# Feed-forward gate by seven block products instead of eight, in a two-layer decoder block

## The chip, the core and the metric

The kernel runs on one core of one Trainium2 chip. The metric is the device time of one execution in microseconds (us). Of three runs of the kernel before, the median is 2764.52 us (2763.65 to 2766.2). The engines are TensorE (PE in the profile; its weight loads PEld), VectorE (DVE), ScalarE (ACT), GpSimd (POOL) and SyncE (SP), which issues every load and store of this kernel on one queue (SPq).

## The reference, cut to what matters

Two decoder layers over 256 tokens with 2048 channels: a token mixer (retention in layer 0, a convolution module in layer 1), a feed-forward part, and a gated per-layer embedding. The change concerns the feed-forward part, which both layers have:

```python
def swiglu(hn, w_gate, w_up, w_down):
    return (jax.nn.silu(hn @ w_gate) * (hn @ w_up)) @ w_down

# in each layer i, h is (256, 2048), FFN_HIDDEN = 5632:
f = swiglu(rms_norm(h, g_ffn_pre[i]), ffn_w_gate[i], ffn_w_up[i], ffn_w_down[i])
h = h + rms_norm(f, g_ffn_post[i])
```

## The kernel before, in words

Everything is float32 at the boundary. Each operand of a matrix product is split into a high part, rounded to the reduced type fp32r, and a low part (the value minus the high part, again fp32r), and a product is three matmuls (`mm3`, L119 to L122): high by high, high by low, low by high. The weights come from memory as tiles of 256 rows by 512 columns (512 KB, `st`, four buffers). `wload` (L75 to L85) issues the load on SP, copies it to the high part `wh` on ACT (L79) and subtracts to the low part `wl` on DVE (L84); `wh` and `wl` have eight buffers each. The activations lie transposed in SBUF as stationary operands: quarters of 4 x 128 channels, high and low, for both token tiles (TT = 2 tiles of 128 tokens), which class `Act` hands out.

`gemm` (L131 to L176) makes 512 output columns for both token tiles: eight weight tiles of two K tiles each, for each K tile both token tiles, three matmuls for each, so 16 x 2 x 3 = 96 matmuls of 128x128 by 128x512. With `outer=True` it goes through all K for token tile 0 first and then for token tile 1 with the weights kept, so that the second tile's activations may come later. Hooks put other work behind a given weight tile.

`ffn` (L588 to L628) walks the 5632 hidden columns in eleven blocks of 512, in groups of 3, 4 and 4 blocks. For each block it makes the gate product, evicts it with a Silu on ACT (L603), makes the up product, multiplies on DVE (L607), transposes the result on TensorE and splits it (`split_to`, L105) into the hidden activations. After each group the down product goes over the group's hidden columns for each of four blocks of 512 outputs: the first group is copied to `y` on ACT (L498), the second added on DVE (L624), the last one added, squared and summed, and scaled (`make_final`, L525). The residual stream `ht` (eight tiles of 128x512) stays in SBUF in a pool `hp` from the end of the retention mixer to the end of the kernel.

Accumulators in PSUM: four tiles `acc`, two for transposes `tp`, two `sm` for the small products. The order of the instructions on each engine is not that of the text: the framework schedules them at compile time, by program order as the priority and by when it reckons that an operand or a buffer is there. Each engine, and the SP queue, then runs its own list strictly in order and waits on semaphores.

Of the kernel before, what the change touches and what calls it, by code (L numbers as in the profile page):

```python
# [10 lines left out]
F32 = mybir.dt.float32  # L11
# [6 lines left out]
P = 128  # L18
# [23 lines left out]
def block_kernel(ctx: ExitStack, tc: tile.TileContext, x, p, positions, w_in, w_out, w_pw1, b_pw1,  # L42
# [76 lines left out]
    def mm3(ps, xh, xl, wh, wl, first, last):  # L119
        nc.tensor.matmul(ps, lhsT=xh, rhs=wh, start=first, stop=False)  # L120
        nc.tensor.matmul(ps, lhsT=xh, rhs=wl, start=False, stop=False)  # L121
        nc.tensor.matmul(ps, lhsT=xl, rhs=wh, start=False, stop=last)  # L122
# [8 lines left out]
    def gemm(act, w, k0, c0, nkt, name, outer=False, hooks=None, on_done=None, hooks1=None, pair=None):  # L131
# [44 lines left out]
        return acc  # L176

# [396 lines left out]

    ssqs = post_setup()
    for c in range(NC):
        if c == 1:
            ret.close()
            hp = ctx.enter_context(tc.tile_pool(name="hp", bufs=1))
            for tt in range(TT):  # L580
                for cc in range(NC):
                    t = ht[tt, cc] = hp.tile([P, CW], F32, tag=f"h{tt}{cc}", name=f"h{tt}{cc}")
                    nc.sync.dma_start(t, x[0, tt * P:(tt + 1) * P, cc * CW:(cc + 1) * CW])
        gemm(yT[1], wo, D, c * CW, NKT, "wo", outer=(c == NC - 1), hooks=hk if c == 0 else None,
             on_done=make_final(c, ssqs, g_mix_post[0], ret_after))


    def ffn(layer, s_hid, after):  # L588
        wg, wu, wd = w_gate[layer], w_up[layer], w_down[layer]
        es = ExitStack()  # L590
        fp = es.enter_context(tc.tile_pool(name=f"ffn{layer}", bufs=1))
        f0 = 0
        groups = (3, 4, 4)
        ssqs = post_setup()
        for gi, n in enumerate(groups):
            hid = Act(s_hid, f"hid{layer}{gi}")
            for j in range(n):
                c0 = (f0 + j) * CW
                sgs, hids = {}, {}

                def gate_done(tt, ps):
                    sgs[tt] = fp.tile([P, CW], F32, tag=f"sg{tt}", name="fsg")
                    nc.scalar.activation(sgs[tt], ps, AF.Silu, scale=rf[layer, tt])  # L603

                def up_done(tt, ps):
                    hids[tt] = fp.tile([P, CW], F32, tag=f"hid{tt}", name="fhid")
                    nc.vector.scalar_tensor_tensor(hids[tt], ps, rf[layer, tt], sgs[tt], op0=ALU.mult, op1=ALU.mult)  # L607

                gemm(fa[layer], wg, 0, c0, NKT, "fg", outer=(gi == 0 and j == 0), on_done=gate_done,
                     hooks={0: pend} if j > 0 else None)  # L610
                gemm(fa[layer], wu, 0, c0, NKT, "fu", on_done=up_done)

                def pend(j=j, hids=hids, hid=hid):
                    for tt in range(TT):
                        split_to(hid, j, tt, transpose4(hids[tt]))
            for c in range(NC):
                last = gi == len(groups) - 1
                if last:
                    done = make_final(c, ssqs, g_ffn_post[layer], after)
                elif gi == 0:  # L620
                    done = first_group_done(c)
                else:
                    def done(tt, ps, c=c):
                        nc.vector.tensor_tensor(y[tt, c], ps, y[tt, c], op=ALU.add)  # L624
                gemm(hid, wd, f0 * CW, c * CW, 4 * n, "fd", outer=(last and c == NC - 1),
                     on_done=done, hooks={1: pend} if c == 0 else None)
            f0 += n
        es.close()  # L628
# [277 lines left out]
    ple(1, final_out)  # L906

# [74 lines left out]
```

## Time and profile before

| | |
|---|---|
| median of three runs | 2764.52 us |
| the profiled execution's own time | 2762.31 us |
| its span, first to last instruction | 2760.5 us |
| PE busy | 2726.0 us (99%), 12288 matmuls |
| DVE busy | 1548.9 us (56%) |
| ACT busy | 1248.4 us (45%) |
| DMA | 521.76 MB, mean 189 GB/s |
| granted TensorE clock | 0.997 of full speed |

A row of a group of instructions reads: line, engine, operation, output and inputs by the program's names, shapes, count; then busy time in us and mean duration of one in ns; then the idle time of that engine just before them and what ended it. Matmuls are pipelined: one shows as 0.39 us and the next begins before it ends, so that the distance from start to start is what one costs. A row of a table of stretches has the stretch and its length, then for each engine busy time and count, then the granted clock, the DMA engines' mean busy share and the rate in GB/s.

### The profile page before, as it was taken

What the parts mean: (1) busy time and instruction counts of PE and PEld (TensorE: products, weight loads), DVE (VectorE), ACT (ScalarE), POOL (GpSimd) and SP (SyncE); (2) the same over time, 40 slices, a digit from 0 to 9 for tenths busy, and PEclk for the clock granted to TensorE, in tenths of its full rate; (3) what the DMA queues carried; (4) which work ended last, traced back from release to release, by engine and by line L of the source; (5) the groups of instructions that cost most, each with busy time, mean ns of one, the idle gap of its engine ahead of it and who ended that gap; (6) DMA issues with size and microseconds to landing.
All of it is one profiled execution on the core that took longest, in us unless ns stands there. A gap on an engine that the chain in (4) does not pass through costs nothing. (4 is left out here: it accounts for less than half of the span.)

```text
span 2760.5 us, 32081 instructions
## 1 busy us (share of the span) xinstructions
PE 2726.0 (99%) x12288; PEld 2249.9 (82%) x12288; DVE 1548.9 (56%) x1701; ACT 1248.4 (45%) x1498; POOL 36.7 (1%) x45
## 2 busy tenths in 40 slices
PE   9999999999999999999999999989999999999998
PEld 7888888888888888888888877878888888888877
DVE  7655545555565445454456577766554445454564
ACT  5444444444454444434444554465444443444453
POOL 0000000000000000000000000000000000000000
PEclk9999999999999999999999999999999999999999
DMA  8666566666576666566655665545756665666653
GB/s 265 195 179 181 183 194 183 181 180 202 168 221 192 190 191 187 192 194 190 189 199 168 206 205 167 163 152 183 226 190 191 191 189 192 192 190 191 202 183 122
DMA packets 293082, 521.76 MB, mean 189 GB/s; under 512 B 18156, under 2 KB 61004, under 8 KB 292928
## 3 DMA queue, kind: packets, MB, share of 16 engines
q1 hardware_dynamic: 292928, 519.72, 60.5%
q8 instruction: 96, 1.57, 0.2%
q14 instruction: 58, 0.48, 0.1%
HBM read 517.55 MB, written 2.10 MB: 188 GB/s over the span
## 5 line engine op out<-in xcount | busy, mean ns | idle before, releaser
L84 DVE TENSOR_TENSOR wl<-st,wh 128x1024 fp32r<-128x1024 f32 x944 | 1154.2, 1224 | 1076.3 <-ACT wh L79 1071.8
L79 ACT CAST wh<-st 128x1024 fp32r<-128x1024 f32 x944 | 993.4, 1053 | 1286.1 <-PE fu L122 268.6
L120 PE MATMUL fg<-wh,h_fa 128*128 128x512 f32 x704 | 275.4, 392 | 0.0
L120 PE MATMUL fd<-wh,h_hid 128*128 128x512 f32 x704 | 274.9, 391 | 0.0
L121 PE MATMUL fg<-wl,h_fa 128*128 128x512 f32 x704 | 274.4, 390 | 0.1
L122 PE MATMUL fg<-wh,l_fa 128*128 128x512 f32 x704 | 274.4, 390 | 0.0
L122 PE MATMUL fd<-wh,l_hid 128*128 128x512 f32 x704 | 274.2, 390 | 0.0
L121 PE MATMUL fd<-wl,h_hid 128*128 128x512 f32 x704 | 273.9, 389 | 0.0
L120 PE MATMUL fu<-wh,h_fa 128*128 128x512 f32 x704 | 273.9, 389 | 0.0
L121 PE MATMUL fu<-wl,h_fa 128*128 128x512 f32 x704 | 273.9, 389 | 0.0
L122 PE MATMUL fu<-wh,l_fa 128*128 128x512 f32 x704 | 273.9, 389 | 0.0
L121 PEld LDWEIGHTS fg<-wl,h_fa 128*128 128x128 f32 x704 | 132.2, 188 | 27.5 <-DVE wl L84 1.0
L122 PEld LDWEIGHTS fd<-wh,l_hid 128*128 128x128 f32 x704 | 132.2, 188 | 27.5
L121 PEld LDWEIGHTS fu<-wl,h_fa 128*128 128x128 f32 x704 | 132.2, 188 | 27.5
L120 PEld LDWEIGHTS fu<-wh,h_fa 128*128 128x128 f32 x704 | 132.2, 188 | 27.4
L122 PEld LDWEIGHTS fu<-wh,l_fa 128*128 128x128 f32 x704 | 132.2, 188 | 27.4
L122 PEld LDWEIGHTS fg<-wh,l_fa 128*128 128x128 f32 x704 | 132.2, 188 | 27.2
L121 PEld LDWEIGHTS fd<-wl,h_hid 128*128 128x128 f32 x704 | 132.2, 188 | 27.1
L120 PEld LDWEIGHTS fg<-wh,h_fa 128*128 128x128 f32 x704 | 132.2, 188 | 26.9
L120 PEld LDWEIGHTS fd<-wh,h_hid 128*128 128x128 f32 x704 | 132.2, 188 | 26.8
L120 PE MATMUL v<-wh,h_x 128*128 128x512 f32 x256 | 101.4, 398 | 0.0
L121 PE MATMUL v<-wl,h_x 128*128 128x512 f32 x256 | 100.6, 393 | 0.5 <-DVE wl L313 0.5
(241 smaller groups left out, 3823.6 us busy)
## 6 DMA issues: line engine op xcount, KB each, us to landing
st<-in_ffn_w_gate_dram SPq DMA_DIRECT2D x176, 512.0 KB, 3.7
st<-in_ffn_w_up_dram SPq DMA_DIRECT2D x176, 512.0 KB, 4.3
st<-in_ffn_w_down_dram SPq DMA_DIRECT2D x176, 512.0 KB, 3.6
st<-in_ret_w_in_dram SPq DMA_DIRECT2D x128, 512.0 KB, 3.8
st<-in_conv_w_pw_dram SPq DMA_DIRECT2D x80, 512.0 KB, 5.4
st<-in_ret_w_in_dram SPq DMA_DIRECT2D x128, 256.0 KB, 3.0
st<-in_ret_w_out_dram SPq DMA_DIRECT2D x64, 512.0 KB, 3.6
st<-in_ple_w_gate_dram SPq DMA_DIRECT2D x64, 512.0 KB, 3.9
```

What stands on the lines that cost most here:

```text
L79: nc.scalar.copy(wh, st)
L84: nc.vector.tensor_tensor(wl, st, wh.bitcast(F32), op=ALU.subtract)
L120: nc.tensor.matmul(ps, lhsT=xh, rhs=wh, start=first, stop=False)
L121: nc.tensor.matmul(ps, lhsT=xh, rhs=wl, start=False, stop=False)
L122: nc.tensor.matmul(ps, lhsT=xl, rhs=wh, start=False, stop=last)
```

## The change

The gate product of the first block of 512 columns stays plain. The other ten blocks go in five pairs. A pair's gate product is a 2 x 2 block product (two token tiles by two halves of K, times two halves of K by two blocks of 512 columns), made with seven block products in the Strassen-Winograd form: four sums S1 to S4 of activation blocks are made once for each layer (`sums`, for a quarter of K at a time, with the normalizing row scale put in first because the blocks mix the two token tiles), and four differences of weight blocks are made in each pair on DVE from unsplit weight tiles (`raw`, four buffers). Each of the seven has 8 K tiles, 24 matmuls. The pieces alternate with the up product of the pair's two blocks and with the down product of the hidden columns of the pair before (eight K tiles, four for the first block), so the down product is added to `y` after each pair. The hidden activations take half of the activation buffers, S1 and S2 the other half; the residual tiles are written to a tensor in device memory behind the first gate block, their SBUF goes to the new tiles, and they are read back in the last down product.

The core of the diff (`+` lines of the new `ffn`; helpers of a few lines left out at `...`):

```diff
+    def gemm_outer(act, w, k0, c0s, nkt, name, dones):
+        ws = {}
+        for tt in range(TT):
+            at = 0
+            for c0, done in zip(c0s, dones):
+                acc = acc_tile(f"{name}{tt}")
+                for su in range(nkt // 2):
+                    if tt == 0:
+                        ws[c0, su] = wload(wsrc(w, k0 + su * 256, c0))
+                    wh, wl = ws[c0, su]
+                    for r in range(2):
+                        kt = su * 2 + r
+                        mm3(acc, *act.get(tt, kt), wh[:, r, :], wl[:, r, :], kt == 0, kt == nkt - 1)
+                    if at >= 2:
+                        step()
+                    at += 1
+                done(tt, acc)
...
-        groups = (3, 4, 4)
...
+        gemm(A, wg, 0, 0, NKT, "fg", outer=True, on_done=gate_done)
+        parked = {}
+        for tt in range(TT):
+            for c in range(NC):
+                t = parked[tt, c] = park.tile([P, CW], F32, tag=f"p{layer}{tt}{c}", name=f"p{layer}{tt}{c}")
+                nc.sync.dma_start(t, ht[tt, c])
+        hp.close()
+        raw = es.enter_context(tc.tile_pool(name=f"raw{layer}", bufs=4))
+        def norm_rows():
+            for tt in range(TT):
+                f = t512("rb")[:, 0:P]
+                nc.scalar.activation(f, ident, AF.Identity, scale=0.0, bias=rf[layer, tt])
+                tp = tpp.tile([P, 4, P], F32, tag="tp", name="tp")
+                nc.tensor.transpose(tp[:, 0, :], f, ident)
+                rrow[tt] = fp.tile([P, P], F32, tag=f"r{tt}", name="rrow")
+                nc.vector.tensor_copy(rrow[tt], tp[:, 0, :])
+        def sums(q):
+            ... # block: hi + lo; scale: times rrow; put: split into S[i]
+            a21, a22, a11, a12 = block(1, q), block(1, q + 2), block(0, q), block(0, q + 2)
+            nc.vector.tensor_tensor(a22, a21, a22, op=ALU.add)
+            scale(a22, 1)
+            put(1, a22)
+            scale(a11, 0)
+            scale(a21, 1)
+            nc.vector.tensor_tensor(a21, a11, a21, op=ALU.subtract)
+            put(3, a21)
+            nc.vector.tensor_tensor(a11, a22, a11, op=ALU.subtract)
+            put(2, a11)
+            scale(a12, 0)
+            nc.vector.tensor_tensor(a12, a12, a11, op=ALU.subtract)
+            put(4, a12)
+        def single(ps, op, half, c0, first):
+            for su in range(HK // 2):
+                wh, wl = wload(wsrc(wg, half * HK * P + su * 256, c0))
+                for r in range(2):
+                    kt = su * 2 + r
+                    mm3(ps, *op(kt), wh[:, r, :], wl[:, r, :], first and kt == 0, kt == HK - 1, not first)
+        def split(t):
+            wh = wpool.tile([P, 2, CW], F32R, tag="wh", name="wh")
+            nc.scalar.copy(wh, t)
+            wl = wpool.tile([P, 2, CW], F32R, tag="wl", name="wl")
+            nc.vector.tensor_tensor(wl, t, wh.bitcast(F32), op=ALU.subtract)
+            return wh, wl
+        def differences(ps, su, c0):
+            b = {}
+            for i, (half, n) in enumerate(((0, 0), (0, 1), (1, 1), (1, 0))):
+                t = b[half, n] = raw.tile([P, 2, CW], F32, tag="raw", name="raw")
+                wdma(t, wsrc(wg, half * HK * P + su * 256, c0 + n * CW))
+            ... # product: split(t), then 2 K tiles x mm3 into ps[key]; sub: DVE subtract
+            sub(b[0, 0], b[0, 1], b[0, 0])
+            product(5, b[0, 0], s_op(1))
+            sub(b[0, 1], b[1, 1], b[0, 1])
+            product(7, b[0, 1], s_op(3))
+            sub(b[1, 1], b[1, 1], b[0, 0])
+            product(6, b[1, 1], s_op(2))
+            sub(b[1, 0], b[1, 0], b[1, 1])
+            product(4, b[1, 0], lambda kt: A.get(1, HK + kt))
...
+        gemm(A, wu, 0, 0, NKT, "fu", on_done=up_done, hooks={0: norm_rows, 2: lambda: sums(0)})
+        todo = [lambda tt=tt, t=gated[tt]: to_hidden(0, tt, t) for tt in range(TT)]
+        k0, nkt, done = 0, 4, first_group_done
+        f0 = 1
+        while f0 < FF // CW:
+            b1 = acc_tile("m1")
+            single(b1, lambda kt: A.get(0, kt), 0, c0, True)
+            m1 = gpool.tile([P, CW], F32, tag="g", name="m1")
+            nc.scalar.activation(m1, b1, AF.Copy, scale=r0)
+            for f in todo:
+                f()
+            down(k0, nkt, 0, done(0))
+            single(b1, lambda kt: A.get(0, HK + kt), 1, c0, False)
+            nc.scalar.activation(g[0, 0], b1, AF.Silu, scale=r0)
+            if first:
+                sums(1)
+            down(k0, nkt, 1, done(1))
+            ps = {i: acc_tile(f"m{i}") for i in (5, 7, 6, 4)}
+            differences(ps, 0, c0)
+            down(k0, nkt, 2, done(2))
+            differences(ps, 1, c0)
+            down(k0, nkt, 3, done(3))
+            differences(ps, 2, c0)
+            up = pair("fu")
+            plain(A, wu, 0, c0, range(NKT // 2), up, NKT)
+            ... # times g[0, 0]; up[1] to u1
+            differences(ps, 3, c0)
+            up = pair("fu")
+            plain(A, wu, 0, c0 + CW, range(0, 3), up, NKT)
+            to_hidden(0, 0, g[0, 0])
+            ... # five DVE operations and two Silu: m1, g[1, 1], g[0, 1]
+            plain(A, wu, 0, c0 + CW, range(3, 5), up, NKT)
+            single(ps[5], s_op(4), 1, c0 + CW, False)
+            ... # g[1, 0] on DVE, Silu
+            to_hidden(0, 1, g[0, 1])
+            plain(A, wu, 0, c0 + CW, range(5, NKT // 2), up, NKT)
+            ... # times g[1, tt]
+            todo = [lambda tt=tt, t=g[1, tt]: to_hidden(1, tt, t) for tt in range(TT)]
+            k0, nkt, done = c0, 8, add_done
+            f0 += 2
+        def last_hidden():
+            for f in todo:
+                f()
+            es.close()
+            open_residual(lambda tt, c: parked[tt, c])
+        gemm(hid, wd, k0, 0, nkt, "fd", hooks={0: last_hidden}, on_done=finals[0])
+        gemm(hid, wd, k0, CW, nkt, "fd", on_done=finals[1])
+        gemm_outer(hid, wd, k0, (2 * CW, 3 * CW), nkt, "fd", finals[2:])
```

`plain` is the plain product over given weight tiles, `down` a plain product of the hidden columns with `w_down` for 512 outputs, `to_hidden` transposes and splits 512 hidden columns of one token tile, `pair` takes both `sm` tiles.

## Rows read from the trace of the kernel before

**Rows 1.** Page: busy time, share of span and instructions of each engine
```profile
PE 2726.0 (99%) x12288; PEld 2249.9 (82%) x12288; DVE 1548.9 (56%) x1701; ACT 1248.4 (45%) x1498; POOL 36.7 (1%) x45
```
**Rows 2.** Waits of PE within layer 0's feed-forward stage (us, times, longest)
```profile
PE tp L116 <- DVE h L553: 0.3, 1, 0.3
```
**Rows 3.** Timeline of PE in layer 0's first up product (start, length)
```profile
781.40 0.39 PE L120 MATMUL fu<-wh,h_fa 128*128 128x512 f32 x1
781.62 0.39 PE L121 MATMUL fu<-wl,h_fa 128*128 128x512 f32 x1
...
792.28 0.39 PE L120 MATMUL fu<-wh,h_fa 128*128 128x512 f32 x1
```
**Rows 4.** Stretches: feed-forward, and the kernel's opening (columns as described above)
```profile
0.00:30.00 30.00, 23.11 (x99) 18.71 (x100) 17.70 (x25) 14.10 (x19) 0.70 (x6) 1.00 0.84 281
30.00:60.00 30.00, 30.00 (x134) 24.78 (x133) 25.99 (x50) 20.30 (x33) 2.89 (x2) 1.00 0.82 258
757.00:780.00 23.00, 22.71 (x108) 18.43 (x107) 19.99 (x29) 13.51 (x23) 3.78 (x3) 1.00 0.62 191
780.00:803.00 23.00, 23.00 (x103) 19.02 (x103) 14.28 (x13) 11.89 (x12) 0.00 (x0) 1.00 0.83 268
803.00:847.00 44.00, 44.00 (x200) 36.52 (x199) 21.69 (x20) 19.10 (x20) 0.00 (x0) 1.00 0.66 190
```
**Rows 5.** Groups of instructions by line, whole kernel
```profile
L84 DVE TENSOR_TENSOR wl<-st,wh 128x1024 fp32r<-128x1024 f32 x944 | 1154.2, 1224 | 1076.3 <-ACT wh L79 1071.8 <-DMA h<-in_x_dram 1.5 <-DMA st<-in_conv_w_pw_dram 1.5
L79 ACT CAST wh<-st 128x1024 fp32r<-128x1024 f32 x944 | 993.4, 1053 | 1286.1 <-PE fu L122 268.6 <-PE fd L122 246.7 <-PE fg L122 233.3
L607 DVE SCALAR_TENSOR_TENSOR fhid<-fu,rstd,fsg 128x512 f32<-128x512 f32 x44 | 30.9, 744 | 0.0
L603 ACT ACTIVATE fsg<-fg,rstd 128x512 f32<-128x512 f32 x44 | 30.1, 688 | 25.3 <-PE fg L122 25.3
L109 DVE TENSOR_TENSOR l_hid<-tp,h_hid 128x512 fp32r<-128x512 f32 x44 | 28.2, 683 | 0.0
L538 DVE TENSOR_TENSOR y<-y,g 128x512 f32<-128x512 f32 x32 | 21.1, 687 | 4.3 <-ACT junk L193 4.3
L624 DVE TENSOR_TENSOR y<-fd,y 128x512 f32<-128x512 f32 x16 | 10.3, 683 | 0.0
```
**Rows 6.** DMA issues: KB each, median us from issue to landing
```profile
st<-in_ffn_w_gate_dram SPq DMA_DIRECT2D x176, 512.0 KB, 3.7
```
**Rows 7.** Timeline of ACT, end of the first gate product
```profile
778.44 1.05 ACT L79 CAST wh<-st 128x1024 fp32r<-128x1024 f32 x1 [1.75 <-DMA st<-in_ffn_w_up_dram]
779.72 1.06 ACT L79 CAST wh<-st 128x1024 fp32r<-128x1024 f32 x1 [0.22 <-DMA st<-in_ffn_w_up_dram]
781.13 1.05 ACT L79 CAST wh<-st 128x1024 fp32r<-128x1024 f32 x1 [0.36 <-DMA st<-in_ffn_w_up_dram]
782.09 0.68 ACT L603 ACTIVATE fsg<-fg,rstd 128x512 f32<-128x512 f32 x1
```
**Rows 8.** Timeline of DVE there
```profile
772.26 3.49 DVE L84 TENSOR_TENSOR wl<-st,wh 128x1024 fp32r<-128x1024 f32 x3
776.72 1.23 DVE L84 TENSOR_TENSOR wl<-st,wh 128x1024 fp32r<-128x1024 f32 x1 [0.96 <-ACT wh L79]
779.52 2.51 DVE L84 TENSOR_TENSOR wl<-st,wh 128x1024 fp32r<-128x1024 f32 x2 [1.58 <-ACT wh L79]
782.22 1.23 DVE L84 TENSOR_TENSOR wl<-st,wh 128x1024 fp32r<-128x1024 f32 x1 [0.19 <-ACT wh L79]
```
**Rows 9.** Waits of the SP queue, whole kernel (us, times, longest)
```profile
SPq L68 <- DVE wl L84: 1921.2, 842, 13.2
```
**Rows 10.** Stretches in which PE paused: the mixer of layer 1, the kernel's end
```profile
1820.00:1830.00 10.00, 7.54 (x33) 5.12 (x31) 8.30 (x17) 4.50 (x7) 0.00 (x0) 1.00 0.73 248
1830.00:1840.00 10.00, 7.74 (x33) 5.73 (x34) 4.60 (x8) 7.75 (x22) 0.55 (x1) 0.83 0.10 38
2755.00:2760.00 5.00, 0.00 (x0) 0.00 (x0) 2.07 (x4) 0.00 (x0) 0.00 (x0) 0.55 0.56 210
```

More of the change, by code (lines that the diff above doesn't have):

```diff
@@ L117, in transpose4, with mm3 @@
         return tp
[L119 to L122, printed above, removed]
+    def mm3(ps, xh, xl, wh, wl, first, last, more=False):
+        nc.tensor.matmul(ps, lhsT=xh, rhs=wh, start=first, stop=False, skip_group_check=more)
+        nc.tensor.matmul(ps, lhsT=xh, rhs=wl, start=False, stop=False, skip_group_check=more)
+        nc.tensor.matmul(ps, lhsT=xl, rhs=wh, start=False, stop=last, skip_group_check=more)
     steps = []
@@ L578, in block_kernel @@
             ret.close()
[L579 to L583, printed above, removed]
+            open_residual(lambda tt, c: x[0, tt * P:(tt + 1) * P, c * CW:(c + 1) * CW])
         gemm(yT[1], wo, D, c * CW, NKT, "wo", outer=(c == NC - 1), hooks=hk if c == 0 else None,
@@ L590, in ffn @@
         es = ExitStack()
         fp = es.enter_context(tc.tile_pool(name=f"ffn{layer}", bufs=1))
-        f0 = 0
-        groups = (3, 4, 4)
[L594 to L627, printed above, removed]
@@ new lines, in ffn, with view, block, scale @@
+        for i, q in ((1, 2), (2, 3), (3, None), (4, None)):
+            if q is not None:
+                S[i] = [apool.tile([P, TT, 4, P], F32R, tag=f"{k}{s_hid}{q}", name=f"s{k}{i}") for k in "hl"]
+            else:
+                S[i] = [fp.tile([P, TT, 4, P], F32R, tag=f"s{k}{i}", name=f"s{k}{i}") for k in "hl"]
+        def sums(q):
+            def view(t):
+                return t.rearrange("p (k n) -> p k n", n=P)
+            def block(tt, q):
+                f = view(t512("sf"))
+                hi, lo = A.quarter(q)
+                nc.vector.tensor_tensor(f, hi[:, tt].bitcast(F32), lo[:, tt].bitcast(F32), op=ALU.add)
+                return f
+            def scale(f, tt):
+                nc.vector.tensor_tensor(f, f, rrow[tt].unsqueeze(1).broadcast_to([P, 4, P]), op=ALU.mult)
+            def put(i, f):
+                hi, lo = S[i]
+                nc.scalar.copy(hi[:, q], f)
+                nc.vector.tensor_tensor(lo[:, q], f, hi[:, q].bitcast(F32), op=ALU.subtract)
+            a21, a22, a11, a12 = block(1, q), block(1, q + 2), block(0, q), block(0, q + 2)
[11 more added lines that the diff above has]
+            put(4, a12)
@@ new lines, in differences, with product, sub @@
+        def differences(ps, su, c0):
[3 more added lines that the diff above has]
+                wdma(t, wsrc(wg, half * HK * P + su * 256, c0 + n * CW))
+            def product(key, t, op):
+                wh, wl = split(t)
+                for r in range(2):
+                    kt = su * 2 + r
+                    mm3(ps[key], *op(kt), wh[:, r, :], wl[:, r, :], kt == 0, kt == HK - 1)
+            def sub(o, x, y):
+                nc.vector.tensor_tensor(o, x, y, op=ALU.subtract)
+            sub(b[0, 0], b[0, 1], b[0, 0])
[6 more added lines that the diff above has]
+            product(4, b[1, 0], lambda kt: A.get(1, HK + kt))
@@ new lines, in to_hidden, with down, add_done, f @@
+        def to_hidden(j, tt, t):
+            split_to(hid, j, tt, transpose4(t))
+        def down(k0, nkt, c, done):
+            acc = pair("fd")
+            plain(hid, wd, k0, c * CW, range(nkt // 2), acc, nkt)
+            for tt in range(TT):
+                done(tt, acc[tt])
+        def add_done(c):
+            def f(tt, ps):
+                nc.vector.tensor_tensor(y[tt, c], ps, y[tt, c], op=ALU.add)
+            return f
+        gemm(A, wu, 0, 0, NKT, "fu", on_done=up_done, hooks={0: norm_rows, 2: lambda: sums(0)})
@@ L631, in block_kernel @@
+        finals = [make_final(c, ssqs, g_ffn_post[layer], after) for c in range(NC)]
+        def last_hidden():
[6 more added lines that the diff above has]
+        gemm_outer(hid, wd, k0, (2 * CW, 3 * CW), nkt, "fd", finals[2:])
     pa = [Act(0, "pa0"), Act(1, "pa1")]
```

50 lines of the change are left out of this document (49 added, 1 removed).

## The prediction

> **What bounds the kernel now.** First the page's busy shares: TensorE has 2726.0 of 2760.5 us, VectorE 56%, ScalarE 45% [rows 1]. A busy TensorE need not be a full one, so next the waits: in layer 0's whole feed-forward stage TensorE waited 0.3 us, once [rows 2]. Then the timeline, for what a matmul costs: 48 of them lie between the starts at 781.40 and 792.28, so 10.88 / 48 = 0.2267 us each [rows 3]. A block of 512 hidden columns has 96 gate and 96 up matmuls, 192 x 0.2267 = 43.5 us, and the stretches show 44.0 us for it with its eight transposes (0.06 us each) and TensorE busy throughout [rows 4]. The stage is a chain of matmuls without gaps: time leaves it only by fewer matmuls, and comes in wherever the other engines can't keep up. In that stretch VectorE works 21.7 of 44 us and the DMA engines 66% at 190 GB/s [rows 4]; that is the room the change spends.
>
> **What goes.** A pair of gate blocks took 192 matmuls and takes 7 x 24 = 168. Five pairs, two layers: 240 fewer, x 0.2267 = 54.4 us. The up and down products keep their counts, and so do the hidden transposes; the row scale adds four transposes in all, 4 x 0.06 = 0.2 us. Every new product is a 128x128 by 128x512 matmul as before, so I give it the same 0.2267 us.
>
> **What VectorE gets, in a later pair.** Weight tiles to split: 12 for the plain block products, 16 for the differences, 16 up, 16 down, 60 x 1.224 = 73.4 us [rows 5]. Subtractions of raw weight tiles: 16, of the shape of the low-part subtraction but with a plain float32 output, which the trace has only at half the size (0.687 us for 512 columns, against 0.683 with the reduced type, L538 and L109 [rows 5]): so 1.224, 19.6 us. Additions to `y`: 8 x 0.683 = 5.5. Joining the products: 5 x 0.685 and 4 x 0.744, 6.4. Hidden low parts 4 x 0.683 = 2.7. Together 107.6 us. TensorE in the same pair: 552 x 0.2267 + 16 x 0.06 = 126.1 us. That is 85% for VectorE. The opening shows that such a load can run: from 30 to 60 us VectorE is busy 25.99 of 30 (87%), ScalarE 20.30, DMA 258 GB/s, and TensorE all 30 [rows 4]. The DMA need here is 60 x 0.524 MB = 31.5 MB in 126.1 us, 249 GB/s; the rate at a full share is about 268 / 0.83 = 323 GB/s [rows 4]. ScalarE has 60 x 1.053 plus some 12 evictions and copies at 0.6 to 0.7, 71 us, and bounds nothing [rows 5].
>
> The tight place of a later pair is from the first differences to the third, with two downs between. TensorE: 72 + 96 matmuls, 38.1 us. VectorE: 24 x 1.224 for differences, 8 x 1.224 and 4 x 0.683 for the downs, 41.9 us. But the eight weight buffers let it come in with four difference tiles and four down tiles done (12 x 1.224 = 14.7 us), and after its last one TensorE still has six matmuls, 1.4 us: 41.9 - 14.7 + 1.4 = 28.6 of 38.1. So 9.5 us of cover; I charge 0.5 us for each of the eight later pairs, 4 us, with 0 and 5 each as ends (5 if half the lead is missing and VectorE runs at the 87% above).
>
> **The first pair of a layer** has no such cover. Its downs have four K tiles, half as long, and the sums of activations fall here: 16 operations for each half of K, 32 x 0.687 = 22.0 us. From the start of the first up product to the end of the third differences TensorE has 96 + 9 x 24 = 312 matmuls and 8 transposes, 71.2 us. VectorE: low parts for 5 up tiles (about three are made when the product starts at 781.40 [rows 8]), 8 plain, 8 down and 12 difference tiles, 33 x 1.224 = 40.4; raw subtractions 12 x 1.224 = 14.7; sums 22.0; up evictions 2 x 0.744 and hidden low parts 2 x 0.683, 2.9. Together 80.0 us, and 1.4 us for the last six matmuls: TensorE waits 80.0 + 1.4 - 71.2 = 10.2 us. The first sums can move into the 2.7 us that VectorE idles before (0.96 + 1.58 + 0.19 [rows 8]): 7.5. I take 8 us for each layer, 16. Ends: 1.4 us if all eight up tiles are ready as well (5 x 1.224 less), 22 us if VectorE runs at 87% (80.0 / 0.87 = 92.0).
>
> **Parking the residual.** Eight writes of 256 KB, 2.1 MB, 6.5 us at 323 GB/s, on the one SP queue among the up tiles' loads, in the place where ScalarE already waits for those loads (1.75, 0.22, 0.36 us [rows 7]). What is queued behind a parking store are the next weight loads, then the splits, then the first up product. TensorE has a tile in hand there, 2.7 us. Value 1.5 us a layer, 3 in all; ends 0 and 6.5 each. Reading back starts once the last pair's tiles are free and has about 32 us of down products (144 matmuls) before the first use: nothing. The last down product is 8 K tiles for each of four blocks, with the last two blocks done token tile by token tile: its tail after the last matmul is as before.
>
> **The sum**, against the profiled execution's 2762.3 us (2760.5 of span and 1.8 around it): - 54.4 + 0.2 + 16 + 4 + 3 = -31.2, so 2731.1. The median lies 2.2 us over that execution: **2733 us**, 1.1% faster.
>
> **Rivals.**
>
> (1) *All of it hidden.* The compiled order may let VectorE reach further ahead than I reckon, since it isn't the text's: the copies for up tiles stand ahead of the gate's Silu [rows 7]. Then 2708.1 + 2 x 1.4 + 2.2 = 2713 us, with 2708 to 2720 around it. Against it: 80 us of VectorE work are due in 71 whatever the order.
>
> (2) *The raw loads come late: slower.* SP runs its list strictly in order and its weight loads wait for a buffer that VectorE frees, 842 times before [rows 9]. There are only four raw buffers, all used in each differences. If the next four loads stand behind the down's four, 8 x 0.524 MB / 323 GB/s = 13.0 us, and some 2 us of latency (3.7 us to landing, 1.6 of it transfer [rows 6]) make 15 us from release to the last landing. With 9.8 us of VectorE behind that, one round takes 24.9 us; TensorE's (24 + 48 matmuls) takes 16.3. Three rounds miss 25.8 us, less at most 14.7 of lead: 11 us a pair, 110 in all, and 2733 + 110 = 2843. With one late round of the three it is nothing in later pairs and 8.6 us in each first one. It turns the sign from 3.1 us for each of ten pairs on. For it: four buffers, one queue. Against it: two of the four raw tiles are free about 4 us before the differences end, and DMA has 25% to spare.
>
> (3) *TensorE's clock falls in the pauses.* From 1820 to 1840 us TensorE paused 2.46 and 2.26 us in two slices of 10, and its granted clock fell to 0.83 in the second, that is to the lower level (1.2 GHz instead of 2.4) for part of it: 0.17 x 10 = 1.7 us lost. At the end, with TensorE idle, the mean is 0.55 [rows 10]. The first pairs' waits come in pieces of about that size, one for each of three differences. Six such losses are 10 us, 2743; if the differences of both first pairs run wholly at the lower level, 2 x 72 x 0.2267 = 33 us, 2766. The Trainium skill ("TensorE: Matmul & The Clock Gate", section on HAM oscillation in real kernels) has the rule: the half clock is the default, activity lifts it, and a kernel that waits for data in every K tile can start every one at half clock. By that rule the time would be at this rival's upper end; the first row agrees only for a part, since the clock held at 1.00 in the slice with the longer pause.
>
> (4) *The pieces don't alternate as written.* If the compiler put three differences together, VectorE's 29.4 us would stand against 16.3 of TensorE, up to 13 us a pair, 2840. Nothing in the trace speaks for it.
>
> **Chances.** The forecast 0.50 (2720 to 2745), (1) 0.16, (2) 0.18, (3) 0.08, (4) 0.03, the rest 0.05. A measurement of this kernel tells a change from none at about 0.2%, 5.5 us. Faster: 0.50 + 0.16, from (2) 0.04 with one late round, from (3) 0.06, from the rest 0.03: 0.79. Same: 0.06, the upper end of (3), the middle of (2) and part of the rest. Slower: 0.15, most of (2) and (4). Range for 8 in 10: 2710 (all hidden but the smallest waits) to 2760 (22 us in each first pair is 2761); the forecast's own range is 2720 to 2745.
>
> **What would show it.** Matmul starts 0.2267 us apart within each product, 240 fewer of them. Waits of TensorE's differences products for low parts: near 8 us in the first pair of each layer, under 1 us in a later pair. VectorE about 97% busy in the first pair and 85% in a later one; 249 GB/s in a later pair. Rival (2) would show as subtractions of raw tiles that wait for a DMA, (3) as slices with a granted clock under 0.9, (4) as differences back to back in the timeline. I am wrong if a later pair takes more than 130 us, or if the first pair waits less than 3 us or more than 16.

## The result and the profile after

The changed kernel takes 2722.74 us (median of four runs, 2718.06 to 2724.3), the kernel before 2764.09 beside it (2763.55 to 2766.2). The ratio is 0.985, 95% interval 0.983 to 0.986: 1.5% faster, 41 us, where the forecast was 1.1%, 2733. The profiled execution took 2721.54 us, its span 2719.8 (2760.5 before).

By stages, from the start of the first gate matmul to that of the last down matmul: layer 0's feed-forward part went from 732.8 to 710.5 us, layer 1's from 733.2 to 713.4. Without any wait each would have lost 120 x 0.2267 = 27.2 us; they lost 22.3 and 19.8. The other stages together are 1.3 us longer.

The busy shares of the page, against [rows 1]: 400 us more VectorE, 136 more ScalarE.

```profile
PE 2679.2 (99%) x12052; PEld 2206.5 (81%) x12052; DVE 1948.7 (72%) x2147; ACT 1384.7 (51%) x1658; POOL 41.2 (2%) x45
```

The page's groups of the operations that the change added or kept, against [rows 5]; the last number is idle time before them:

```profile
L84 DVE TENSOR_TENSOR wl<-st,wh 128x1024 fp32r<-128x1024 f32 x904 | 1096.4, 1222 | 521.6 <-ACT wh L79 512.4
L740 DVE TENSOR_TENSOR raw<-raw 128x1024 f32<-128x1024 f32 x160 | 195.4, 1221 | 104.6 <-DMA raw<-in_ffn_w_gate_dram 102.7
```

The subtraction of raw tiles (L740) takes 1.221 us, as priced from its neighbours. VectorE waits 102.7 us in all for raw tiles to land: its own idle time, which by itself costs TensorE nothing. Three stretches: a later pair, 127 us; the first pair of layer 0 from its transposes on, 110 us; and in layer 0 the place for which the prediction added up VectorE's work, from the first up product to the end of the third differences (columns as in [rows 4]):

```profile
918.00:1045.00 127.00, 127.00 (x569) 105.15 (x568) 102.53 (x98) 68.75 (x73) 0.00 (x0) 1.00 0.76 250
808.00:918.00 110.00, 107.65 (x486) 88.55 (x485) 97.88 (x97) 67.00 (x77) 0.00 (x0) 1.00 0.79 259
780.60:855.50 74.90, 72.55 (x323) 59.44 (x323) 71.80 (x81) 46.52 (x56) 0.00 (x0) 1.00 0.73 240
```

In the later pair TensorE has no wait, DMA runs at 250 GB/s (249 were reckoned), and VectorE is busy 102.5 of 127 us: 81%, not 85%. Over the whole first pair it is 89%; but the 97% that were forecast were those of the reckoned place, and there it is busy 71.8 of 74.9 us, 96% (in layer 1 72.7 of 78.5, 93%). So the share came true, but not its terms: what is due there is less and cheaper (68.0 us, below), and VectorE goes on into the next product's tiles. Why VectorE has less to do than the sum of its operations is in a row of three in its timeline, which [rows 8] already had:

```profile
769.04 1.22 DVE L84 TENSOR_TENSOR wl<-st,wh 128x1024 fp32r<-128x1024 f32 x1
770.17 1.29 DVE L109 TENSOR_TENSOR l_fa<-pf,h_fa 128x512 fp32r<-128x512 f32 x2
771.38 0.14 DVE L207 TENSOR_SCALAR s<-s 128x1 f32<-128x1 f32 x1
771.44 3.48 DVE L84 TENSOR_TENSOR wl<-st,wh 128x1024 fp32r<-128x1024 f32 x3
```

One takes 1.22 us, and three take 3.48: 1.13 from start to start (the 512-column ones 0.60, not 0.68). An operation's last 0.09 us overlap with the next. The Trainium skill ("Perfetto Trace Analysis", section Optimizing Scalar/DVE Operations) says the same in general: a part of a profiled VectorE operation lies beside the next one. The trace agrees, with 0.09 us of 1.22.

**Where TensorE waits.** Of the ten pairs only the first of each layer waits (0.4 us once in another). Layer 0, timeline of TensorE (start, length, idle before and its releaser); the eight transposes are those of the first block's hidden activations, `m` before and after them the pair's first and second plain product, `fd` the first down product:

```profile
808.11 1.04 PE L116 MATMUL tp<-ident,fsg 128*128 128x128 f32 x8
810.11 0.50 PE L121 MATMUL m<-wh,h_fa 128*128 128x512 f32 x1 [0.97 <-ACT m L779]
...
812.96 0.50 PE L123 MATMUL fd<-wh,l_hid 128*128 128x512 f32 x1 [1.38 <-DVE l_hid L109]
```

The second plain product goes on in the accumulator of the first, so it may only begin when ScalarE has copied that out (L779). Layer 1, the same place:

```profile
1945.14 1.04 PE L116 MATMUL tp<-ident,fsg 128*128 128x128 f32 x8
1949.61 0.80 PE L121 MATMUL m<-wh,h_fa 128*128 128x512 f32 x1 [3.43 <-ACT m L779]
1950.20 0.63 PE L122 MATMUL m<-wl,h_fa 128*128 128x512 f32 x1
1950.63 0.63 PE L121 MATMUL fd<-wh,h_hid 128*128 128x512 f32 x1
...
1955.24 0.48 PE L122 MATMUL fd<-wl,h_hid 128*128 128x512 f32 x1
1955.56 0.39 PE L123 MATMUL fd<-wh,l_hid 128*128 128x512 f32 x1
1955.79 0.39 PE L121 MATMUL fd<-wh,h_hid 128*128 128x512 f32 x1
```

After 3.43 us of waiting the matmuls come 0.43 us apart (some 0.6) until 1955.3, and 0.227 again from there, which adds 3 us to the wait: 13 distances take 5.95 us where 13 x 0.2267 is 2.95. The stretch shows the granted clock at 0.50, the lower level (columns as in [rows 4]):

```profile
1950.00:1955.00 5.00, 5.00 (x12) 3.44 (x12) 4.44 (x9) 3.13 (x5) 0.00 (x0) 0.50 0.77 277
```

What held the copy up is a chain over VectorE, the SP queue, the DMA engines and ScalarE. In layer 0, in this order: timeline of VectorE, of the SP queue (start, then how long issuing took), the SP queue's waits for low parts from 780 to 800 us (us, times, longest), two stretches (columns as in [rows 4]), and the timeline of ScalarE:

```profile
785.01 1.28 DVE L683 TENSOR_TENSOR sf<-h_fa,l_fa 128x512 f32<-128x512 f32 x2
786.21 1.89 DVE L687 TENSOR_TENSOR sf<-sf,rrow 128x512 f32<-128x512 f32 x3
...
791.08 0.68 DVE L705 TENSOR_TENSOR sf<-sf 128x512 f32<-128x512 f32 x1
791.69 1.22 DVE L84 TENSOR_TENSOR wl<-st,wh 128x1024 fp32r<-128x1024 f32 x1
```

```profile
782.07 11.26 SPq L68 DMA_DIRECT2D st<-in_ffn_w_gate_dram  x4
795.31 1.50 SPq L68 DMA_DIRECT2D st<-in_ffn_w_down_dram  x2
797.58 7.46 SPq L68 DMA_DIRECT2D st<-in_ffn_w_gate_dram  x4
```

```profile
SPq L68 <- DVE wl L84: 16.1, 8, 7.8
```

```profile
787.00:797.00 10.00, 10.00 (x46) 8.27 (x45) 10.00 (x14) 4.89 (x8) 0.00 (x0) 1.00 0.35 115
797.00:802.00 5.00, 5.00 (x24) 4.14 (x23) 4.16 (x6) 1.91 (x2) 0.00 (x0) 1.00 0.87 291
```

```profile
796.80 1.05 ACT L79 CAST wh<-st 128x1024 fp32r<-128x1024 f32 x1 [4.38 <-DMA st<-in_ffn_w_gate_dram]
...
808.43 1.05 ACT L79 CAST wh<-st 128x1024 fp32r<-128x1024 f32 x1 [1.10 <-DMA st<-in_ffn_w_gate_dram]
809.38 0.68 ACT L779 ACTIVATE m<-m,rstd 128x512 f32<-128x512 f32 x1
```

From 785.01 to 791.69 VectorE works on the first half of the sums without a break, while tiles that ScalarE has already cast wait for their low parts (L84). A tile that waits keeps its stage buffer, so the SP queue waits for a low part for up to 7.8 us and takes 11.26 us to issue four loads; the DMA rate falls to 115 GB/s for 10 us and then runs at 291; ScalarE waits 4.38 us for a tile, and for each of the next ones; the copy of the first product stands in its list behind seven such casts and ends at 810.06, 1.2 us after TensorE is through with the transposes (they and the switch take 0.79). VectorE is busy in all of those 10 us, and the wait that TensorE shows for it names ScalarE.

Layer 0's second wait, 1.38 us for a low part of the hidden activations (L109), has a shorter cause: two operations of the second half of the sums stand ahead of it on VectorE.

```profile
811.01 0.68 DVE L695 TENSOR_TENSOR sf<-sf 128x512 f32<-128x512 f32 x1
811.62 0.68 DVE L687 TENSOR_TENSOR sf<-sf,rrow 128x512 f32<-128x512 f32 x1
812.22 1.28 DVE L109 TENSOR_TENSOR l_hid<-tp,h_hid 128x512 fp32r<-128x512 f32 x2
```

### The profile page after: what moved, and what is told of

It reads as the page before. It is cut to its first block, busy times and chain, and to the rows that moved or that the text cites. A ratio compares the mean times of both kernels' runs of the same rounds, so it can differ in the third digit from the quotient of the medians.

```text
span 2719.8 us, 32681 instructions
## 1 busy us (share of the span) xinstructions
PE 2679.2 (99%) x12052; PEld 2206.5 (81%) x12052; DVE 1948.7 (72%) x2147; ACT 1384.7 (51%) x1658; POOL 41.2 (2%) x45
## 4 chain that ended last, share of the span: by engine, by line
PE 86%; DVE 6%; DMA 5%; ACT 1%; issue 1%; POOL 1%; SPq 0%; DVEq 0%; POOLq 0%; ACTq 0%
PE fu L121 5%; PE fu L123 5%; PE fu L122 5%; PE fd L123 5%; PE fd L122 5%; PE fd L121 5%; PE m L121 4%; PE m L122 4%; PE m L123 4%; PE v L122 2%; PE v L123 2%; PE v L121 2%; PE g L121 2%; PE g L123 2%; PE g L122 2%; PE qk L121 2%
## 5 line engine op out<-in xcount | busy, mean ns | idle before, releaser
L79 ACT CAST wh<-st 128x1024 fp32r<-128x1024 f32 x904 | 949.7, 1052 | 1038.2 <-PE fd L123 198.8
L84 DVE TENSOR_TENSOR wl<-st,wh 128x1024 fp32r<-128x1024 f32 x904 | 1096.4, 1222 | 521.6 <-ACT wh L79 512.4
L740 DVE TENSOR_TENSOR raw<-raw 128x1024 f32<-128x1024 f32 x160 | 195.4, 1221 | 104.6 <-DMA raw<-in_ffn_w_gate_dram 102.7
L721 ACT CAST wh<-raw 128x1024 fp32r<-128x1024 f32 x160 | 166.1, 1049 | 73.9 <-DVE raw L740 34.8
L723 DVE TENSOR_TENSOR wl<-raw,wh 128x1024 fp32r<-128x1024 f32 x160 | 189.5, 1219 | 11.3 <-ACT wh L721 7.7
L123 PEld LDWEIGHTS fd<-wh,l_hid 128*128 128x128 f32 x704 | 132.6, 188 | 29.9 <-DVE l_hid L109 2.4
L122 PE MATMUL m<-wl,sh 128*128 128x512 f32 x320 | 125.3, 392 | 0.0
L121 PE MATMUL m<-wh,sh 128*128 128x512 f32 x320 | 125.0, 390 | 0.0
L123 PE MATMUL m<-wh,sl 128*128 128x512 f32 x320 | 124.4, 389 | 0.0
```

What stands on the lines that cost most here:

```text
L79: nc.scalar.copy(wh, st)
L84: nc.vector.tensor_tensor(wl, st, wh.bitcast(F32), op=ALU.subtract)
L721: nc.scalar.copy(wh, t)
L723: nc.vector.tensor_tensor(wl, t, wh.bitcast(F32), op=ALU.subtract)
L740: nc.vector.tensor_tensor(o, x, y, op=ALU.subtract)
```

## Experiments

Below, "excess" of a pair is worked out from the trace: over all distances above 0.36 us from one TensorE start to the next, the sum of what they have over 0.227; so it holds the waits and the matmuls at the lower clock. The changed kernel has 2.6 us in layer 0's first pair, 6.4 in layer 1's, and 0.4 in the eight later pairs together.

| kernel | median, us | ratio to before, interval | excess of the first pairs, layer 0, 1 | of eight later pairs |
|---|---|---|---|---|
| the change | 2722.74 | 0.985, 0.983 to 0.986 | 2.6, 6.4 | 0.4 |
| without sums | 2721.70 | 0.984, 0.983 to 0.986 | 2.2, 1.2 | 0.9 |
| without parking | 2722.44 | 0.985, 0.983 to 0.987 | 3.0, 6.2 | 0.2 |
| an eighth product | 2774.89 | 1.004, 1.002 to 1.005 | 2.4, 5.8 | 0 |
| copy first | 2727.50 | 0.986, 0.985 to 0.988 | 3.7, 4.9 | 4.5 |
| two low parts more | 2725.87 | 0.986, 0.984 to 0.987 | 5.2, 6.3 | 0 |
| four low parts more | 2752.97 | 0.995, 0.993 to 0.997 | 12.6, 15.3 | 3.5 |
| differences in a row | 2847.09 | 1.029, 1.028 to 1.031 | 19.8, 18.2 | 88.5 |
| three raw buffers | 2756.45 | 0.997, 0.996 to 0.998 | 8.4, 12.5 | 21.5 |
| two accumulators | 2725.39 | 0.986, 0.984 to 0.987 | 7.8, 5.9 | 0.3 |
| two accumulators, no sums | 2723.70 | 0.984, 0.983 to 0.986 | 4.3, 6.3 | 0 |
| half the sums behind | 2725.94 | 0.986, 0.984 to 0.987 | 6.8, 6.8 | 0.4 |
| all sums behind | 2728.96 | 0.987, 0.986 to 0.989 | 8.2, 7.0 | 0 |

**Is TensorE the bound of every pair?** The second plain product's matmuls are made twice, 24 more a pair.

```diff
-            single(b1, lambda kt: A.get(0, HK + kt), 1, c0, False)
+            single(b1, lambda kt: A.get(0, HK + kt), 1, c0, False, 2)
...
-                    mm3(ps, *op(kt), wh[:, r, :], wl[:, r, :], first and kt == 0, kt == HK - 1, not first)
+                    for _ in range(times):
+                        mm3(ps, *op(kt), wh[:, r, :], wl[:, r, :], first and kt == 0, kt == HK - 1, not first)
```

> The second block product's matmuls are issued twice with the same weights (the result is then not the reference's): 24 more matmuls in each of ten pairs, as many as an eighth product would have, and no work for other engines. If TensorE bounds every later pair, each matmul saved is worth its 0.2267 us: 2722.7 + 54.4 = 2777 us, less up to 9 where a first pair's wait is covered. If another engine bounded the later pairs (a rival to the step that costs them at nothing), less than 40 us would come back.

It costs 52.2 us of the 54.4 that the matmuls take, and a later pair goes from 127.1 to 132.6 us. So what the change removes is paid out at its full price.

**Parking.** The eight stores a layer are left out, and another tensor is read back.

```diff
-                nc.sync.dma_start(t, ht[tt, c])
+                parked[tt, c] = x[0, tt * P:(tt + 1) * P, c * CW:(c + 1) * CW]
```

> Leaves out the parking stores (the residual is read back from the input x, so that the loads stay). Theory A: the time stays, 2722 within 2 us, with the same waits in the first pairs. Rival B (stores delay the weight loads there): waits go, 2713 to 2716 us. Rival C: as A.

No change in the time, nor in either stage (710.7 and 713.4 us). The parking stores cost nothing that can be measured; the reading back stayed in.

**The sums left out.** The unsummed blocks stand in for S1 to S4, and the row scale goes too.

```diff
-            return lambda kt: tuple(t[:, kt // 4, kt % 4, :] for t in S[i])
+            return (lambda kt: A.get(0, HK + kt)) if i == 4 else (lambda kt: A.get(1, kt))
...
-        gemm(A, wu, 0, 0, NKT, "fu", on_done=up_done, hooks={0: norm_rows, 2: lambda: sums(0)})
+        gemm(A, wu, 0, 0, NKT, "fu", on_done=up_done)
```

> Leaves out the activation sums and the row scale (the products take unsummed activation blocks), so 22 us of VectorE work per layer are gone from the stretch before the first pair's differences; matmuls, loads and splits stay. Theory A (VectorE's sums hold back the low parts, thereby the stage buffers, the loads and, through ScalarE's list, the copy of the first block product that TensorE waits for): the waits in the first pairs of 3 and 6 us go, 2722.7 - 9 - 1 = 2713 us. Rival B (the parking stores on the SP queue and DMA): the waits stay, 2721 or more. Rival C (only that the copy stands behind seven casts in ScalarE's list): some of it stays, 2718 to 2721.

The whole hardly moves (2721.7, where theory A said 2713), but the stages do: 709.2 and 708.9 us, 1.3 and 4.5 less, and the slow stretch of layer 1 is gone. It is given back in layer 0's embedding, whose order came out differently (108.6 us instead of 104.8). So most of layer 1's loss goes with the sums. The 2.2 and 1.2 us that stay can't be put down to a cause by this run alone, for without the sums VectorE's order came out differently: the four subtractions of raw tiles for the first differences, which the change makes long before (from 696 and 1816 us), here fall beside the first up product, ahead of low parts, and wait for loads (L734 in this kernel; layer 1):

```profile
1934.78 1.23 DVE L734 TENSOR_TENSOR raw<-raw 128x1024 f32<-128x1024 f32 x1 [2.20 <-DMA raw<-in_ffn_w_gate_dram]
```

**The order on ScalarE and TensorE.** Two edits let the copy, or the second product, come earlier: the second product's casts behind the copy on ScalarE, and in the first pair an accumulator of its own for the second product, made before the hidden transposes.

```diff
+            with tc.issue_after(m1_copy.ins):
+                single(b1, lambda kt: A.get(0, HK + kt), 1, c0, False)
```

> The casts of the second block product's weights are put behind the copy of the first block product in ScalarE's list, in every pair; nothing else changes. Rival C (the copy's place is the whole cause): the first pairs' waits go, 2714 us. Theory A (VectorE is behind anyway): the wait for the copy goes, but a part comes back as waits for low parts, 2716 to 2721 us. Rival B: no change, 2722.

```diff
+            if first:
+                b2 = acc_tile("m2")
+                single(b2, lambda kt: A.get(0, HK + kt), 1, c0, True)
             for f in todo:
                 f()
...
+                nc.vector.scalar_tensor_tensor(g[0, 0], b2, r0, m1, op0=ALU.mult, op1=ALU.add)
+                nc.scalar.activation(g[0, 0], g[0, 0], AF.Silu)
```

> In the first pair of each layer the second block product goes to an accumulator of its own and directly behind the first, ahead of the transposes of the first hidden block; one more VectorE operation adds the two. Theory D (the first pair's wait is a chain of dependences: the end of the first up product, gating, transposes, casts, low parts, first down matmul, with only 24 matmuls to cover it): with 48 to cover it the waits of 2.5 and 3.4 us go and with them the lower clock behind the second, 2722.7 - 3 - 6 = 2714 us. Theory A (VectorE is behind by its sums): the waits move to the differences, no gain, 2720 to 2724.

Neither is faster (by the medians they are 3 to 5 us slower, with intervals that overlap the change's), and the first pair's wait only changes its name. TensorE's waits, of the first and of the second of these (us, times, longest):

```profile
PE fd L121 <- ACT h_hid L108: 6.9, 2, 3.5
```

```profile
PE m L121 <- ACT wh L721: 7.1, 4, 2.9
```

The first run's time, 2727.5, is above what any of its theories said: the edit is made in every pair, and the later pairs now lose 4.5 us too. In the second run the waits stand at the differences, as its theory A said, and its time, 2725.4, is just above that theory's range. The copy was the last in a line of late things, not the cause. The second of these edits together with the sums left out:

> Leaves out the activation sums and the row scale (the unsummed blocks stand in for S1 to S4), and gives the second plain product of the first pair an accumulator of its own right behind the first. Theory E (two things hold up the first pair, either one enough to make a wait: VectorE's work on the sums, and the copy of the first product that stands behind the second product's casts on ScalarE): with both gone the first pairs wait under 1 us a layer; feed-forward stages 707 to 709 us in both layers, and the whole at 2714 to 2720 us (the embedding of layer 0 may again cost 3.8 us, as in the run without sums alone). Theory F (what waits is the chain from the last up matmul over gating, transposes, casts and low parts to the first down, which no reordering shortens): at least 1.5 us of wait a layer stay, just before the first down product; stages 709 to 712 us, the whole 2720 to 2725 us.

The waits stay, 4.3 and 6.3 us, so theory E falls, and theory F's numbers nearly fit (2723.7; layer 1's stage, 712.6 us, is just past its range). But VectorE's timeline there shows another reason than F's, the one of the run without sums: a subtraction of raw tiles (L734) has taken the place of the sums, stands ahead of low parts and waits for its load (layer 1):

```profile
1941.22 1.23 DVE L734 TENSOR_TENSOR raw<-raw 128x1024 f32<-128x1024 f32 x1 [4.92 <-DMA raw<-in_ffn_w_gate_dram]
```

**Where the sums stand.** The chain shown for layer 0 says that the first half of the sums, beside the up product, does the harm. First the other half is moved behind the low parts of the hidden activations, then both halves.

```diff
             if first:
-                sums(1)
+                with tc.issue_after(low.ins):
+                    sums(1)
```

> The second half of the sums (11 us of VectorE) stands behind the low parts of the hidden activations that the first down product needs, instead of wherever it fits before. Theory H (in the first pair the sums stand ahead of low parts on VectorE; those hold the stage buffers, the loads and with them ScalarE's casts come late, and the first product's copy behind the casts comes late): the waits around the hidden transposes shrink from 3.0 and 6.3 us to under 1 us in layer 0 and under 3 in layer 1, half of VectorE's surplus shows up later, at the second or third differences, 0 to 3 us a layer; stages 707 to 710 and 707 to 712 us, the whole 2715 to 2721 us. Theory F (the chain from the last up matmul through gating, transposes, casts and low parts is what waits, whoever else works): the waits stay, and 2 to 4 us come on top at the differences, 2722 to 2729 us.

The time is 2725.9 where theory H said 2715 to 2721. TensorE waits 4.0 and 4.4 us at the old place, and with the matmuls at the lower clock behind them the excess is 6.8 us in each layer. Only layer 0's wait for the low part of the hidden activations is gone. The half left beside the up product now runs unbroken in layer 1 too, and the DMA engines stand still (stretch of layer 1, columns as in [rows 4]):

```profile
1930.00:1935.00 5.00, 5.00 (x23) 4.13 (x22) 5.00 (x8) 3.37 (x5) 0.00 (x0) 1.00 0.01 2
```

This edit moved the wrong half: it is the first that holds the buffers.

```diff
-        gemm(A, wu, 0, 0, NKT, "fu", on_done=up_done, hooks={0: norm_rows, 2: lambda: sums(0)})
+        gemm(A, wu, 0, 0, NKT, "fu", on_done=up_done, hooks={0: norm_rows})
...
+                with tc.issue_after(low.ins):
+                    sums(0)
...
             differences(ps, 0, c0)
+            if first:
+                with tc.issue_after(low.ins):
+                    sums(1)
```

> Both halves of the sums stand behind those low parts, so nothing of them runs beside the up product. Theory H: no wait of more than 1 us before the first down product in either layer, and no slow stretch of matmuls there; but then VectorE has the sums (22 us), 24 low parts of weight tiles (29.4 us, less a lead of eight, 9.8), two subtractions of raw tiles for each differences past the first (9.8) and 1.4 us of hidden low parts, some 53 us, between the first down and the end of the third differences, where TensorE has 192 matmuls, 43.5 us: about 9 us of wait a layer at the differences; 2726 to 2736 us. Theory F: the wait before the first down stays at 1.5 us or more, with those 9 us on top; 2732 to 2742 us.

Now the wait before the first down product is gone in both layers, and so is the half clock there. The SP queue's longest wait for a low part falls from 7.8 to 2.4 us (layer 0, 780 to 800 us as above), in the same stretch of layer 1 the DMA engines run on, and from there ScalarE's casts wait for TensorE to free a buffer, no longer for loads (SP queue, stretch, ScalarE):

```profile
SPq L68 <- DVE wl L84: 14.5, 9, 2.4
```

```profile
1930.00:1935.00 5.00, 5.00 (x24) 4.14 (x23) 3.68 (x3) 2.79 (x3) 0.00 (x0) 1.00 0.79 278
```

```profile
1943.29 1.05 ACT L79 CAST wh<-st 128x1024 fp32r<-128x1024 f32 x1 [1.67 <-PE fu L123]
...
1951.45 0.69 ACT L779 ACTIVATE m<-m,rstd 128x512 f32<-128x512 f32 x1 [0.30 <-PE m L123]
```

That shows the chain's cause, and theory F falls: with the sums taken out from between, and the four raw subtractions made early as in the change (from 695 and 1822 us), every later link goes. But the 22 us of sums are then due in a shorter time, and TensorE waits for VectorE at the second down and at the differences instead:

```profile
1977.06 0.50 PE L122 MATMUL fd<-wl,h_hid 128*128 128x512 f32 x1 [2.30 <-DVE wl L84]
```

With the lower clock behind these waits, 8.2 and 7.0 us are lost, near the 9 expected: 2729 us, 6 more than the change by the medians. No order that was tried beats the change's; the first half alone behind the low parts was not tried.

**How much cover a later pair has.** Two of four low parts, then all four of each differences, are made twice: 9 and 16 us more of VectorE busy in a later pair.

```diff
-            nc.vector.tensor_tensor(wl, t, wh.bitcast(F32), op=ALU.subtract)
+            for _ in range(times):
+                nc.vector.tensor_tensor(wl, t, wh.bitcast(F32), op=ALU.subtract)
```

> Makes two of the four low parts of each differences twice, 9.8 us more VectorE work in each pair, 7.3 us of it in the tight place from the first to the third differences. Theory A (a later pair has some 9.5 us of cover there, as the prediction reckoned, and only the first pairs have none): later pairs without waits, length 127 to 128 us; only the first pairs lose, 2 to 8 us each; 2724 to 2737 us. Rival (VectorE's work costs in proportion from the first microsecond, as with all four doubled, which cost 30 us for 19.6 us a pair): half of that, 15 us, spread over all pairs, 2737 to 2742 us.

> Each low part in the differences is made twice (same result): 4 x 1.22 = 4.9 us more of VectorE in each differences, 19.6 in each pair, 127.2 us against 127.1 of the later pair as measured. Theory (VectorE's share is what limits further steps, the 15% it had left covers the change): TensorE now waits in each later pair, at least 1 and up to 10 us, 2735 to 2820 us. Rival (the cover is not VectorE's time but buffers or loads): no change, 2723 to 2728.

A later pair with all four made twice (columns as in [rows 4]):

```profile
927.00:1054.00 127.00, 127.00 (x569) 104.98 (x568) 118.56 (x114) 65.82 (x70) 0.00 (x0) 1.00 0.76 248
```

With two more the later pairs keep their 127.1 us, as theory A said, and the first pair of layer 0 pays 2.6. With four more VectorE is at 93% in a later pair, and the later pairs' excess is 0.4 us on average, where at least 1 was expected of each; the first pairs pay 10 and 9. Of the 34 us by which its profiled execution is slower these are 19 and the later pairs 3; 5 more lie between the two feed-forward parts, and the rest is not accounted for. So the cover in the tight place is about the 13.6 us (12 x 1.13) that were added there, not 9.5.

**The prices of the two slower rivals.** One raw buffer less; and the four differences back to back.

```diff
-        raw = es.enter_context(tc.tile_pool(name=f"raw{layer}", bufs=4))
+        raw = es.enter_context(tc.tile_pool(name=f"raw{layer}", bufs=3))
```

> Three raw buffers in place of four: the fourth weight block is loaded only when the first one is done with. If the raw loads' round trip is near the limit (the prediction's rival on late raw loads), VectorE loses about 4 us in each differences, 16 in a pair, and of it the tight place misses some 3: 2722.7 + 8 x 3 + 2 x 6 = 2759 us. If the round trip has room to spare, no change: 2723 to 2727.

```diff
-            differences(ps, 0, c0)
-            down(k0, nkt, 2, done(2))
-            differences(ps, 1, c0)
-            down(k0, nkt, 3, done(3))
-            differences(ps, 2, c0)
+            for su in range(4):
+                differences(ps, su, c0)
+            down(k0, nkt, 2, done(2))
+            down(k0, nkt, 3, done(3))
```

> The four differences of a pair stand one behind the other, the downs and the up product behind them; the work is the same. By the prediction's rival on bunched pieces, which counts no lead: 13 us or more for each pair, 2850 us. By the buffers: eight difference tiles can be ready (19.6 us of VectorE), which leaves 39.2 - 19.6 + 1.4 = 21.0 us against TensorE's 21.8, so 0 to 3 us a pair, 2722 to 2755, and with late raw loads (15 us a round) up to 8 a pair, 2800.

Waits with three buffers: VectorE for loads, and TensorE for an accumulator that VectorE empties late:

```profile
DVE raw L740 <- DMA raw<-in_ffn_w_gate_dram: 119.3, 66, 4.2
...
PE fu L121 <- DVE fsg L798: 15.5, 6, 3.4
```

Waits of TensorE with the differences in a row, for their casts and for the accumulators of the downs:

```profile
PE m L121 <- ACT wh L721: 45.4, 25, 2.4
PE fd L121 <- DVE y L762: 15.7, 8, 3.5
```

With three raw buffers 34 us are lost (2756, near the 2759 expected), so four are enough but with little to spare; whether more would help wasn't tried. In a row the differences cost 124 us, 12.4 a pair, and turn the gain into a loss. The expectation that lead in the buffers would cover most of it was wrong. Not all of it is waiting: the granted clock over the whole span falls from 0.995 to 0.983, by an estimate 0.012 x 2847 = 34 us.

## Why the prediction came out as it did

**What goes: right.** 240 matmuls at 0.2267 us; the eighth product put in again costs 52.2 of 54.4.

**The first pair: right in kind, 16 us charged and 9.0 found, and in another place.** The step that failed is "VectorE: low parts for 5 up tiles ..., 33 x 1.224 ... Together 80.0 us", and with it the wait that was to follow at the differences. It priced an operation by its mean length, 1.224, where in a row one costs 1.13; [rows 8] had it (3.49 for three). And it counted four subtractions of raw tiles that the compiled order makes long before: the first differences' tiles have buffers of their own, and VectorE subtracts them at 696 us, in the retention's output product (in layer 1 at 1816). With 1.13 and 0.60, and eight raw subtractions, the work is 37.3 + 9.0 + 19.2 + 2.5 = 68.0 us (the trace has 68.0 from 780.5 to 850.7 us, with 33 low parts and eight raw subtractions), 69.4 with the last matmuls, of TensorE's 71.2: no surplus, and indeed TensorE does not wait for the differences' low parts. What it does wait for the sum could not see: not how much VectorE has to do but what stands ahead of what, with the stage buffers as the link. The forecast's range (3 to 16 us a pair) holds 6.4; layer 0's 2.6 lies just below its lower bound, so by the prediction's own sign that step was wrong there. That layer 1's 6.4 comes near the 8 charged is luck: it is a wait of 3.4 us in another place and 3 us of the lower clock, which the term did not have.

**A later pair: 0.5 us charged each, 4 in all; 0.4 us found in all eight.** Its price of 126.1 us was 127.1, mostly since a transpose costs 0.11 us from start to start and not 0.06. The 0.06 came from a misreading: the 44.0 us of [rows 4] are the length of the stretch that was asked for, while in the trace of before the block takes 44.4, from the gate matmul at 803.2 to the next block's at 847.6. Both kernels have these transposes, so the difference of the two is untouched.

**Parking: 3 us charged, nothing found** when the stores were left out.

**The sum,** profiled execution to profiled execution: -54.4, first pairs +9.0, later pairs +0.4, the wait for the new residual's transposes in layer 0's last down product +0.3 (0.85 us, 0.55 before), other stages +1.3: -43.4, and -40.8 was measured. The 2.6 left lie in distances too short to single out. Against the forecast of -31.2 the first pairs gave 7.0, the later pairs 3.6, parking 3.0.

**The rivals.** All hidden (2713) is 10 us away; 6 of these are the two first pairs (9.0, where it allowed 2.8). Late raw loads: the mechanism is there, VectorE waits 102.7 us for them, but TensorE doesn't, until a buffer is taken away. The falling clock came once, in layer 1, for 3 us. The Trainium skill's rule ("TensorE: Matmul & The Clock Gate", section HAM oscillation — how this bites in real kernels) would have had the differences at half clock; they wait for nothing here, so the runs bear it out only where a pause was really there, and not after each (below). Pieces not alternating: didn't happen. Its price, 2840, came near the 2847 measured in part by luck, since some 34 us of that are the lower clock, which it left out.

## What to carry to other kernels

Price an engine's operations that run in a row by their distance from start to start, not by the mean length of the group; for a balance near 100% the 8% decide. Where an engine's sum fits its time, look next at what its list does to buffers: work without a deadline put ahead of work that frees a stage buffer stops the loads, and the bill arrives some 17 us later under another engine's name (here from 791.7 to 808.9). And let pieces that are heavy for VectorE alternate with pieces that are light: it is worth 12 us a pair here, with the lower clock that came with the waits.

## What the runs showed of the hardware

A single wait of 3.43 us was followed by 5.6 us of matmuls at the lower clock level; with half the sums behind, waits of 4.0 and 4.4 us, one in each layer, were both followed by it as well. In layer 0 of the change, waits of 0.97 and 1.38 us a few matmuls apart were not. But the length of a wait alone does not decide: in the run "copy first" waits of 3.42 and 3.52 us were not followed by it (0.227 us from start to start behind the first few matmuls, granted clock 1.00), and with all sums behind a wait of 2.26 us in layer 0 was, while one of 2.30 us in layer 1 was not, until two more of 0.9 us had come. What decides is not shown here.

In the changed kernel, with DMA at 250 GB/s in a pair, a load of 512 KB of gate weights takes longer to land than the 3.7 us of [rows 6] (median us from issue to landing); whether the rate does it or the loads issued just before is not shown:

```profile
raw<-in_ffn_w_gate_dram SPq DMA_DIRECT2D x160, 512.0 KB, 5.6
st<-in_ffn_w_gate_dram SPq DMA_DIRECT2D x136, 512.0 KB, 4.6
```
